# Starting the output products of a convolution layer before its last two units are finished

## The chip, the cores and the metric

The kernel runs on one core of a Trainium2 chip. The metric is the device time of one execution in microseconds (us). The profile is one execution taken by the hardware profiler; its engines are PE (matrix products; PEld is the loading of the stationary operand), DVE (vector), ACT (scalar activations), POOL (the third elementwise engine) and SP, whose queue issues the transfers (DMA).

## The reference, cut to what matters

Four layers transform 512 latent tokens and 256 context tokens of width 1024. Layers 0 and 3 are attention with low-rank keys, layer 1 is windowed attention, layer 2 is a Hyena layer, a gated long convolution. All end in a product with an output matrix, a norm and a gated residual:

```python
def hyena_mixer(hx, hc, w_in, conv_w, conv_b, ..., filt_bias, w_out, with_ctx_out):
    def run(h):
        p = h @ w_in
        u = short_conv(p[..., :(C_ORDER + 1) * C_WIDTH], conv_w, conv_b)
        gate = p[..., (C_ORDER + 1) * C_WIDTH:]
        v, *gx = jnp.split(u, C_ORDER + 1, axis=-1)
        z = v
        for o in range(C_ORDER):
            z = gx[o] * bidir_long_conv(z, filt[:, 0, o], filt[:, 1, o], filt_bias[o])
        return (z * jax.nn.silu(gate)) @ w_out
...
        x = x + gate_x * rmsnorm(yx, g_post[layer])
```

The last product sums over 1024 channels, so it needs every channel of `z * silu(gate)`.

## The kernel before, in words

**Layer 2.** `layer_C` works channel by channel in eight units of 128 channels, u = 0 to 7, over all 768 tokens. `w_in(u, c)` multiplies the hidden state `h` with the weights of one of four parts c (48 products a call, line 588), into one of the two double PSUM banks `pb`. `short(u, c)` adds the three-tap convolution (ACT line 1490, DVE lines 1495 to 1498). `gated(u)` is `short(u, 2)`, `w_in(u, 3)`, a SiLU (line 1577) and their product on POOL (line 1578). `conv(u, gx, kb, out)` is one long convolution: fold (DVE, 1506 and 1507), six transposes (PE, 1513), a split of each number into a high and a low part (341, 342), a sign flip (DVE, 1517), the forward transform (PE, 1525 and 1529), products with the filter's spectrum (DVE and POOL, 1534 to 1550), the inverse transform (PE, 1558 and 1563), and the sums that write `out` (ACT 1565 and 1566, DVE 1568 and 1569). It uses seven single PSUM banks `pa` in turn out of four, so two convolutions can overlap only in part. The result of unit u goes to `og[:, u]`.

**The tail of layer 2** (lines 1591 to 1617). Units 6 and 7 are interleaved: first convolutions 6a and 7a, then `gated(6)`, then second convolutions 6b (line 1599) and 7b (line 1600), the gate product of unit 6 (line 1601), `gated(7)`, and the gate product of unit 7 (line 1603). Then the blocks of `h` are freed, `self.W.pump(8, 8)` fetches and splits all eight 128-row blocks of the output matrix, the rings are freed, and `w_out_phase` runs.

**The output product.** `w_out_phase` goes over six tiles of 128 tokens. For a tile it splits the tile's columns of `og` into high and low (ACT 613, DVE 614; tile 0 in two pieces, units 0 to 5 and 6 to 7), then multiplies: for each unit k three products times two halves (line 622), 48 for a tile, into one `pb` bank, which `self.s()` hands out in turn. `post` normalizes (ACT 564, POOL 358 and 359, DVE 566, which reads and writes the bank, and 567, which reads it last), and `pre` prepares the next layer's input (eight transposes, line 543, among it).

**Weights.** `Stream` (`self.W`) fetches them in the order wanted. `_dma` (line 211) puts 512 KB into a staging slot of the F arena; `_split` copies the high part with ACT (line 230), takes the low part with POOL or DVE (line 233) and then frees the slot. `take` fetches and splits what is still missing; `cap_d` bounds the staged blocks and `cap_w` the split ones. A slot of the F arena is chosen among the first `turns_f` free ones, counted from the arena's top; the one freed longest ago is taken. With `turns_f = 1` it is always the topmost.

**Where the slots lie.** Following the arena's allocations through `layer_C` in the order of the code: the ring `acts` has blocks at words 6656, 11712 and 12496 of `arena_f` and one in `swing_F`; the last gate product of unit 7, `g7`, lies in the block 12496 to 13268. The ring `kr` of filter spectra holds words 8640 to 11712. As long as `kr` and `acts` are in use, one staging slot of 1024 words is free, at word 3072 of `swing_F`. Behind the layer the topmost slot of `arena_f` is 12736 to 13760, and so overlaps with `g7`'s block.

**What sets the order.** The last lines of `kernel` build the program in a `TileContext` with `schedule_with_timeline_sim=True`. It takes the code's order as a priority and lets an engine go on to later code where earlier code isn't ready. So `gated(7)`, behind 7b in the code, appears in the trace between the steps of 6b. Once built, the order on each engine is fixed.

Of the kernel before, what the change touches and what calls it, by code (L numbers as in the profile page):

```python
# [12 lines left out]
F32 = mybir.dt.float32  # L13
F32R = mybir.dt.float32r
BF16 = mybir.dt.bfloat16
AF = mybir.ActivationFunctionType
ALU = mybir.AluOpType
AX = mybir.AxisListType

P = 128  # L20
D = 1024
KD = 8
NX = 512
NC = 256
T = NX + NC
# [245 lines left out]
class Kern:  # L271
# [317 lines left out]

    W_AT_START = (4, 3, 3)  # L590

    def w_out_phase(self, L, og, wkey, order, last, hook):

        nc = self.nc
        self.W.cap_d, self.turns_f = 1, 1
        ws = [self.W.take((wkey, k), k < KD - 1) for k in range(KD)]
        h = None
        nxt = None if last else (L + 1) % 3
        ogv = og.v(KD, T)
        self.fill_to("g", L)  # L600
        self.turns_f = 6
        self.M.cap_d = self.M.look_d = 0
        xts = [self.load_x(L, order[0])]
        for n, t in enumerate(order):
            final = n == len(order) - 1
            if not final:
                xts.append(self.load_x(L, order[n + 1]))
            xt = xts[n]
            o2 = self.rs(2 * KD * P)
            ov = o2.v(2, KD, P)  # L610
            src = ogv[:, :, P * t:P * t + P]
            for k in (slice(0, 6), slice(6, 8)) if n == 0 else (slice(0, 8),):
                nc.scalar.activation(ov[:, 0, k], src[:, k], AF.Copy)
                nc.vector.tensor_tensor(ov[:, 1, k], src[:, k], ov[:, 0, k].bitcast(F32), op=ALU.subtract)
            if final:
                og.free()
            ys = self.s()
            for k in range(KD):
                wh, wl = ws[k][1]
                for q, (part, wt) in enumerate(((0, wh), (0, wl), (1, wh))):  # L620
                    for hf in range(2):
                        nc.tensor.matmul(ys[:, 512 * hf:512 * hf + 512], ov[:, part, k], wt[:, 0, 512 * hf:512 * hf + 512],  # L622
                                         start=(k == 0 and q == 0), stop=(k == KD - 1 and q == 2))
            o2.free()
            if n == 0:
                g = self.gates_out(L)
                if not last:
                    self.fill_to("ab", L + 1)
            if final:
                for blk, _ in ws:  # L630
                    blk.free()
                if nxt == 2:
                    self.set_swing("F")
                if nxt is not None:
                    self.W.cap_w, self.W.cap_d = self.W_AT_START[nxt], WD
                    self.W.pump(self.W.cap_w + 1, self.W.cap_w)
            self.post(L, t, ys, xt, g)
            if not last:
                if h is None:
                    h = self.h_alloc()  # L640
                self.pre(L + 1, t, xt, h)
            xt.free()
            if n == 1 and nxt == 0:
                self.W.cap_w, self.W.cap_d = 10, 1
                self.W.pump(2, 2)
            if n in (4, 5) and nxt == 2 and self.fillers and self.fillers[0][0] == "g":
                self.fill()
        if nxt is not None:
            self.W.pump(self.W.cap_w + 1, self.W.cap_w)
        for b in g:  # L650
            b.free()
        self.M.cap_d = self.M.look_d = 1
        return h
# [37 lines left out]
    def layer_A(self, L, j, h, ctx_out, last):  # L691
        nc, R, F = self.nc, self.R, self.F
        self.W.cap_w, self.W.cap_d, self.turns_f = 7, 3, 6
        qt = list(range(6)) if ctx_out else list(range(4))
        order = [0, 1, 2, 3, 4, 5]
        TQ = T if ctx_out else NX
        og = self.fl(KD * T)
# [276 lines left out]
            r.free()  # L974
        qr.free()
        kr.free()
        return self.w_out_phase(L, og, ("aw", L), order if not last else qt, last, None)


    def want_B(self, L, j):  # L980
# [21 lines left out]
    def layer_B(self, L, j, h, last):  # L1002
# [241 lines left out]
            r.free()  # L1244
        for x in (q, kx, vb):
            x.free()
        return self.w_out_phase(L, og, ("bw", L), order, last, None)


    def filters(self, j):  # L1250
# [182 lines left out]
    def layer_C(self, L, j, h, last):  # L1433
# [139 lines left out]
        def gated(u, sg=None):  # L1573
            g1 = short(u, 2)
            ps = w_in(u, 3)
            sg = ogv[:, u] if sg is None else sg
            nc.scalar.activation(sg, ps[:, 0:T], AF.Silu)
            nc.gpsimd.tensor_tensor(g1[:, 0:T], g1[:, 0:T], sg, op=ALU.mult)
            return g1
# [16 lines left out]
        conv(v7, g7, k7, ogv[:, 7])  # L1596
        k7 = load_k(15)
        g6 = gated(6, acts.next().ap[:, 0:T])
        conv(z, None, kb, ogv[:, 6])
        conv(ogv[:, 7], None, k7, ogv[:, 7])  # L1600
        nc.vector.tensor_tensor(ogv[:, 6], ogv[:, 6], g6[:, 0:T], op=ALU.mult)
        g7 = gated(7, acts.next().ap[:, 0:T])
        nc.vector.tensor_tensor(ogv[:, 7], ogv[:, 7], g7[:, 0:T], op=ALU.mult)
        for b in h:
            b.free()
        self.W.cap_w, self.W.cap_d = 8, 2
        self.lo_pool = None
        kr.free()
        self.W.cap_d = 3
        self.W.pump(8, 8)  # L1610
        self.lo_pool = True
        for r in (acts, fold, tr, zs, ubs, ybs):
            r.free()
        tb.free()
        tcf.free()
        self.set_swing("R")
        return self.w_out_phase(L, og, ("cw", L), order, last, None)


    def run(self, layers=(0, 1, 2, 3)):  # L1620
# [177 lines left out]
```

## Time and profile before

| what | value |
|---|---|
| median of 3 runs | 1949.14 us (1948.0 to 1954.3) |
| the profiled execution, its own time | 1953.32 us |
| its span, first to last instruction | 1951.5 us |
| mean granted PE clock | 0.984 |
| PE busy | 1820.0 us, 93% |
| DVE, ACT, POOL busy | 1182.5, 812.3, 521.6 us |

Layer 2 lies between about 1010 and 1594 us of the span. A row of the time line or of the chain begins with its start and its length, both in us. The row of a stretch gives, after the stretch's length, the busy time of each engine with the number of its instructions, then the clock that PE was granted, the share of DMA and its GB/s. A row of a group ends with its busy time, the mean ns of one instruction, and the idle time in front of it.

### The profile page before, as it was taken

How to read it: one execution, taken by the hardware profiler on the slowest of the kernel's cores; microseconds unless marked ns; L12 is line 12 of the kernel's file. 1: busy time of each engine (PE TensorE's matmuls, PEld its weight loads, DVE VectorE, ACT ScalarE, POOL GpSimd, SP SyncE). 2: the span in 40 equal slices, each digit the busy share in tenths (PEclk: the TensorE clock that was granted, in tenths of full speed). 3: DMA queues.
4: the chain of work that ended last, by engine and by line, in shares of the span. 5: the costliest groups of instructions: out<-in, count | busy, mean ns of one | idle time of the engine just before them, and what ended most of it. 6: DMA issues, size and time to landing. Idle time of an engine off the chain costs nothing.

```text
span 1951.5 us, 30304 instructions
## 1 busy us (share of the span) xinstructions
PE 1820.0 (93%) x11628; PEld 1576.6 (81%) x11628; DVE 1182.5 (61%) x2364; ACT 812.3 (42%) x1686; POOL 521.6 (27%) x523
## 2 busy tenths in 40 slices
PE   5879799999999899999989899999998998999998
PEld 3557588999988888888868699999987777889986
DVE  6684134787755367676675445566668553477663
ACT  3473132555544255565664422222222343354451
POOL 5561000000213321221231344444445221000120
PEclk9999899999999999999999999999999999999999
DMA  7857521001133112222362622222221335310121
GB/s 214 259 175 226 158 78 31 22 24 43 44 109 117 57 48 83 76 67 67 99 223 103 204 60 85 70 74 76 76 77 60 122 120 154 87 33 23 44 76 54
DMA packets 186356, 186.31 MB, mean 95 GB/s; under 512 B 16600, under 2 KB 164952, under 8 KB 186212
## 3 DMA queue, kind: packets, MB, share of 16 engines
q1 hardware_dynamic: 186212, 184.39, 30.6%
q8 instruction: 91, 1.49, 0.3%
q14 instruction: 53, 0.43, 0.1%
HBM read 160.24 MB, written 24.12 MB: 94 GB/s over the span
## 4 chain that ended last, share of the span: by engine, by line
PE 77%; DVE 10%; DMA 6%; ACT 3%; issue 3%; POOL 1%; SPq 0%; POOLq 0%; DVEq 0%; ACTq 0%
PE pb L588 13%; PE pb L622 11%; PE pa L588 10%; PE pb L873 5%; PE pa L912 4%; PE pa L1068 3%; PE pa L1049 3%; DMA arena_f<-in_w_mod_dram 3%; PE pa L1525 2%; PE pa L1558 2%; PE pa L442 2%; PE pa L898 2%; PE pa L1177 2%; PE pb L577 2%; PE pb L578 2%
## 5 line engine op out<-in xcount | busy, mean ns | idle before, releaser
L588 PE MATMUL pb<-arena_r 128*128 128x512 f32 (+1 forms) x1536 | 293.2, 345 | 8.1 <-DVE arena_f L1498 3.6
L588 PEld LDWEIGHTS pb<-arena_r 128*128 128x128 f32 x1536 | 239.3, 192 | 40.7 <-issue 3.8
L341 ACT ACTIVATE arena_r<-pa 128x384 fp32r<-128x384 f32 (+2 forms) x382 | 175.3, 478 | 198.5 <-PE pa L898 68.2
L342 DVE TENSOR_TENSOR arena_r<-pa,arena_r 128x384 fp32r<-128x384 f32 (+2 forms) x382 | 199.7, 537 | 86.6 <-ACT arena_r L341 84.9
L588 PE MATMUL pa<-arena_r,swing_R 128*128 128x512 f32 (+1 forms) x816 | 165.9, 355 | 0.6 <-DVE arena_r L342 0.4
L588 PEld LDWEIGHTS pa<-arena_r,swing_R 128*128 128x128 f32 x816 | 132.2, 188 | 21.8 <-DVE arena_r L342 0.6
L873 PE MATMUL pb<-arena_r 128*128 128x384 f32 (+1 forms) x720 | 141.4, 337 | 3.0 <-ACT arena_r L341 1.8
L233 POOL TENSOR_TENSOR swing_R<-arena_f,swing_R 128x1024 fp32r<-128x1024 f32 (+1 forms) x33 | 77.1, 2340 | 200.5 <-ACT swing_R L230 150.7
L873 PEld LDWEIGHTS pb<-arena_r 128*128 128x128 f32 x720 | 119.0, 188 | 5.1 <-ACT arena_r L341 2.5
L668 POOL TENSOR_TENSOR arena_f<-arena_f 128x128 f32<-128x128 f32 (+1 forms) x44 | 20.9, 474 | 364.1 <-DVE small L881 180.1
L622 PE MATMUL pb<-arena_r 128*128 128x512 f32 x480 | 115.2, 393 | 0.0
L358 POOL TENSOR_SCALAR small<-small 128x1 f32<-128x1 f32 x68 | 17.8, 262 | 349.1 <-ACT trash L564 135.6
L622 PEld LDWEIGHTS pb<-arena_r 128*128 128x128 f32 x480 | 89.5, 188 | 20.0 <-issue 1.1
L233 POOL TENSOR_TENSOR arena_r<-swing_F,arena_r 128x1024 fp32r<-128x1024 f32 x34 | 84.6, 2492 | 76.0 <-ACT arena_r L230 73.9
L912 PE MATMUL pa<-arena_r 128*128 128x256 f32 x624 | 91.4, 286 | 2.1 <-DVE arena_r L342 2.1
L912 PEld LDWEIGHTS pa<-arena_r 128*128 128x128 f32 x624 | 81.7, 190 | 4.8 <-ACT arena_r L341 2.5
L1068 PE MATMUL pa<-swing_R,arena_r 128*128 128x256 f32 x576 | 80.2, 289 | 5.1 <-DVE arena_f L348 3.8
L877 DVE TENSOR_REDUCE small<-pb 128x1 f32<-128x768 f32 (+1 forms) x80 | 67.5, 846 | 21.6 <-PE pb L873 20.7
L880 ACT ACTIVATE arena_f<-pb,small 128x768 f32<-128x768 f32 (+1 forms) x80 | 65.2, 816 | 32.9 <-DVE small L878 26.5
L1068 PEld LDWEIGHTS pa<-swing_R,arena_r 128*128 128x128 f32 x576 | 72.9, 192 | 7.3 <-DVE arena_f L348 5.2
L442 PE MATMUL pa<-arena_f,cst 128*32 128x256 f32 x744 | 57.0, 407 | 23.3 <-DMA arena_f<-in_w_mod_dram 23.0
L230 ACT ACTIVATE arena_r<-swing_F 128x1024 fp32r<-128x1024 f32 x34 | 36.2, 1063 | 101.5 <-PE pb L588 93.7
(266 smaller groups left out, 4239.6 us busy)
## 6 DMA issues: line engine op xcount, KB each, us to landing
arena_f<-in_w_mod_dram SPq DMA_DIRECT2D x93, 512.0 KB, 4.8
swing_F<-in_c_w_in_dram SPq DMA_DIRECT2D x31, 512.0 KB, 4.1
kd<-arena_f SPq DMA_DIRECT2D x48, 256.0 KB, 3.4
arena_f<-in_a_w_in_dram SPq DMA_DIRECT2D x24, 512.0 KB, 4.2
arena_f<-kd SPq DMA_DIRECT2D x16, 768.0 KB, 4.5
arena_f<-in_b_w_in_dram SPq DMA_DIRECT2D x20, 512.0 KB, 4.2
x<-arena_f SPq DMA_DIRECT2D x18, 512.0 KB, 4.1
arena_f<-in_a_w_out_dram SPq DMA_DIRECT2D x16, 512.0 KB
```

What stands on the lines that cost most here:

```text
L233: eng.tensor_tensor(lo, view, hi.bitcast(F32), op=ALU.subtract)
L341: self.nc.scalar.activation(hi, src, AF.Copy)
L342: self.nc.vector.tensor_tensor(lo, src, hi.bitcast(F32), op=ALU.subtract)
L442: nc.tensor.matmul(ps[32 * j:32 * j + 32, n0:n0 + 256], self.cst[:, 4 * kh + j, :], w[:, j, :], start=(kh == 0), stop=(kh == 1), skip_grou ...
L588: nc.tensor.matmul(out, l, rhs(part, k, i), start=(k == 0 and q == 0), stop=(k == kt - 1 and q == 2))
L622: nc.tensor.matmul(ys[:, 512 * hf:512 * hf + 512], ov[:, part, k], wt[:, 0, 512 * hf:512 * hf + 512], start=(k == 0 and q == 0), stop=(k = ...
L873: nc.tensor.matmul(S[:, 512 * b:512 * b + w], l, r[:, k0 + w * b:k0 + w * b + w], start=(q == 0), stop=(q == 4))
L877: nc.vector.tensor_reduce(mx, Sv, axis=AX.XY, op=ALU.max)
L880: nc.scalar.activation(pr.v(nb, w), Sv, AF.Exp, bias=mx, scale=sc, accum_out=sm)
L912: nc.tensor.matmul(o[:, 0:256], vv[:, a_, kt % 3, P * hh:P * hh + P], ptv[i // nh][:, b_, i % nh], start=(i == 0 and q == 0), stop=(i == n ...
L1049: nc.tensor.matmul(o, l[:, k], self.h_at(h, part, k, t0, n), start=(k == 0 and i == 0), stop=(k == KD - 1 and i == 2))
L1068: nc.tensor.matmul(ps[:, 0:256], self.h_at(h, part, k, P * t, P), w, start=(k == 0 and i == 0), stop=(k == KD - 1 and i == 2))
```

## The change

- The split and the products of one tile become a method, `w_out_tile`, that can do a range of units only.
- `gated(7)` moves ahead of 6b and 7b. The blocks of `h` are freed behind it, so ahead of these convolutions too. The caps become 6 split blocks and 2 staged ones.
- Behind 6b and 7b, but ahead of the two gate products of units 6 and 7, the first six blocks of the output matrix are taken and the products of units 0 to 5 are emitted for the first two tiles. Both `pb` banks hold these partial sums from then on.
- `pump(8, 8)` goes. `kr` is freed only after these products. The last two blocks are taken inside `w_out_phase`, under its `cap_d = 1` and `turns_f = 1`, behind `set_swing("R")`.
- For these two tiles `w_out_phase` adds units 6 and 7; the other four tiles go as before. The other two callers pass nothing and emit what they emitted.

```diff
-    def w_out_phase(self, L, og, wkey, order, last, hook):
+    def w_out_tile(self, og, ws, t, ks, part=None):
+        nc = self.nc
+        ogv = og.v(KD, T)
+        if part is None:
+            o2 = self.rs(2 * KD * P)
+            part = o2, self.s()
+        o2, ys = part
+        ov = o2.v(2, KD, P)
+        src = ogv[:, :, P * t:P * t + P]
+        nc.scalar.activation(ov[:, 0, ks], src[:, ks], AF.Copy)
+        nc.vector.tensor_tensor(ov[:, 1, ks], src[:, ks], ov[:, 0, ks].bitcast(F32), op=ALU.subtract)
+        for k in range(ks.start, ks.stop):
+            wh, wl = ws[k][1]
+            for q, (a, wt) in enumerate(((0, wh), (0, wl), (1, wh))):
+                for hf in range(2):
+                    nc.tensor.matmul(ys[:, 512 * hf:512 * hf + 512], ov[:, a, k], wt[:, 0, 512 * hf:512 * hf + 512],
+                                     start=(k == 0 and q == 0), stop=(k == KD - 1 and q == 2))
+        return part
+
+    def w_out_phase(self, L, og, wkey, order, last, begun=None):
         self.W.cap_d, self.turns_f = 1, 1
-        ws = [self.W.take((wkey, k), k < KD - 1) for k in range(KD)]
+        ws, parts, k0 = begun or ([], [], 0)
+        ws = ws + [self.W.take((wkey, k), k < KD - 1) for k in range(len(ws), KD)]
...
+            if n < len(parts):
+                o2, ys = self.w_out_tile(og, ws, t, slice(k0, KD), parts[n])
+            elif n == 0:
+                part = self.w_out_tile(og, ws, t, slice(0, 6))
+                o2, ys = self.w_out_tile(og, ws, t, slice(6, KD), part)
+            else:
+                o2, ys = self.w_out_tile(og, ws, t, slice(0, KD))
...
         g6 = gated(6, acts.next().ap[:, 0:T])
+        g7 = gated(7, acts.next().ap[:, 0:T])
+        for b in h:
+            b.free()
+        self.W.cap_w, self.W.cap_d = 6, 2
+        self.lo_pool = None
         conv(z, None, kb, ogv[:, 6])
         conv(ogv[:, 7], None, k7, ogv[:, 7])
+
+        ws = [self.W.take((("cw", L), k), k < 3) for k in range(6)]
+        parts = [self.w_out_tile(og, ws, t, slice(0, 6)) for t in order[:2]]
         nc.vector.tensor_tensor(ogv[:, 6], ogv[:, 6], g6[:, 0:T], op=ALU.mult)
-        g7 = gated(7, acts.next().ap[:, 0:T])
         nc.vector.tensor_tensor(ogv[:, 7], ogv[:, 7], g7[:, 0:T], op=ALU.mult)
-        for b in h:
-            b.free()
-        self.W.cap_w, self.W.cap_d = 8, 2
-        self.lo_pool = None
         kr.free()
-        self.W.cap_d = 3
-        self.W.pump(8, 8)
         self.lo_pool = True
...
-        return self.w_out_phase(L, og, ("cw", L), order, last, None)
+        return self.w_out_phase(L, og, ("cw", L), order, last, (ws, parts, 6))
```

More of the change, by code (lines that the diff above doesn't have):

```diff
@@ L590 @@
     W_AT_START = (4, 3, 3)
-    def w_out_phase(self, L, og, wkey, order, last, hook):
+    def w_out_tile(self, og, ws, t, ks, part=None):
[17 more added lines that the diff above has]
+    def w_out_phase(self, L, og, wkey, order, last, begun=None):
         nc = self.nc
         self.W.cap_d, self.turns_f = 1, 1
-        ws = [self.W.take((wkey, k), k < KD - 1) for k in range(KD)]
+        ws, parts, k0 = begun or ([], [], 0)
+        ws = ws + [self.W.take((wkey, k), k < KD - 1) for k in range(len(ws), KD)]
         h = None
         nxt = None if last else (L + 1) % 3
-        ogv = og.v(KD, T)
         self.fill_to("g", L)
@@ L608, in w_out_phase @@
             xt = xts[n]
[L609 to L614, printed above, removed]
+            if n < len(parts):
[5 more added lines that the diff above has]
+                o2, ys = self.w_out_tile(og, ws, t, slice(0, KD))
             if final:
                 og.free()
[L617 to L623, printed above, removed]
             o2.free()
@@ L976, in layer_A @@
         kr.free()
-        return self.w_out_phase(L, og, ("aw", L), order if not last else qt, last, None)
+        return self.w_out_phase(L, og, ("aw", L), order if not last else qt, last)
     def want_B(self, L, j):
@@ L1246, in layer_B @@
             x.free()
-        return self.w_out_phase(L, og, ("bw", L), order, last, None)
+        return self.w_out_phase(L, og, ("bw", L), order, last)
     def filters(self, j):
```

## The prediction

> **What bounds the kernel now.** I read the page first, then a table of stretches over the end of layer 2, the waits there, the chain of work that ended last, and the time line.
>
> ```profile
> span 1951.5 us, 30304 instructions
> ...
> PE 1820.0 (93%) x11628; PEld 1576.6 (81%) x11628; DVE 1182.5 (61%) x2364; ACT 812.3 (42%) x1686; POOL 521.6 (27%) x523
> ```
>
> PE is the bound, 93% busy, so a change can win only where PE stands still or runs slowly. The stretches show where that is around the change:
>
> ```profile
> 1462.00:1492.70 30.70, 29.41 (x202) 26.91 (x200) 24.61 (x37) 8.74 (x13) 13.84 (x11) 1.00 0.14 43
> 1492.70:1521.60 28.90, 20.28 (x107) 15.46 (x105) 24.45 (x33) 9.02 (x15) 15.39 (x10) 0.88 0.34 109
> 1521.60:1594.40 72.80, 72.48 (x322) 57.19 (x322) 37.33 (x47) 30.25 (x52) 13.17 (x23) 1.00 0.33 113
> ```
>
> The first is nearly full: the input products of `gated(7)` fill the holes of 7a and 6b. The third, the output products, is full. In the second, where the end of 6b and all of 7b are left, PE is idle for 28.9 - 20.3 = 8.6 us, and its clock of 0.88 takes another 0.12 x 28.9 = 3.5 us. These 12 us, 0.6% of the time, are all that there is to win. The waits of that stretch are links of the convolution's own chain through DVE, with no other product at hand:
>
> ```profile
> PE pa L1558 <- DVE arena_r L1544: 4.0, 3, 1.8
> ...
> PE pa L1525 <- DVE arena_r L1517: 2.4, 1, 2.4
> ```
>
> **The moved gates.** The chain shows the products of `gated(7)` (line 588) between the steps of 7a and 6b:
>
> ```profile
> 1467.01 0.72 PE pa L1529 x6
> 1467.73 4.83 PE pb L588 x27
> ...
> 1476.05 1.92 PE pa L1558 x16
> 1477.97 0.89 PE pa L1563 x8
> 1478.86 0.22 PE pa L1513 x2
> 1479.08 5.55 PE pb L588 x32
> 1484.63 2.88 PE pa L1525 x24
> ...
> 1502.12 2.90 PE pa L1525 x12
> ```
>
> Before, 6b stands ahead of `gated(7)` in the code, and its forward transform starts at 1484.63. Now `gated(7)` is ahead. What that does to a convolution shows at 6a, which stands behind four `short` calls:
>
> ```profile
> 1412.53 0.28 DVE L1507 TENSOR_TENSOR swing_F<-swing_F 128x128 f32<-128x128 f32 x1
> ...
> 1425.98 0.69 DVE L1548 TENSOR_TENSOR swing_F<-pa,arena_f 128x512 f32<-128x512 f32 x1
> ```
>
> ```profile
> 1433.71 3.48 PE pb L588 x20
> 1437.19 0.66 PE pa L1513 x6
> ```
>
> Its fold is done by 1412.8, and its first banks are read out by 1426.7 (line 1548 of the convolution ahead). Yet its transposes wait until 1437.19, when the input products ahead of them are through. So I take it that 6b now waits for all of `gated(7)`: 96 products at 5.55/32 = 0.174 us are 16.7 us, from 1467.7, with 7a's inverse transform among them (24 x 1.92/16 + 0.89 = 3.8 us). That ends at 1488.2, and 6b's transposes (0.66) at 1488.9. From there to its forward transform I need the split and the sign flip:
>
> ```profile
> 1480.06 2.37 DVE L1517 TENSOR_SCALAR arena_r<-arena_r,sgn 128x1536 fp32r<-128x1536 f32 x1
> ```
>
> Before, the transposes ended at 1479.08 and the flip at 1482.43, 3.4 us later. So 6b's forward transform starts at 1492.3, 7.7 us late. From there to 7b's it took 1502.1 - 1484.6 = 17.5 us, which I keep. The end of 7b:
>
> ```profile
> 1520.47 0.96 DVE L1603 TENSOR_TENSOR arena_f<-arena_f 128x768 f32<-128x768 f32 x1
> ```
>
> ```profile
> 1500.00:1510.00 10.00, 6.28 (x32) 5.28 (x32) 7.59 (x8) 2.71 (x4) 5.37 (x4) 0.83 0.23 62
> 1510.00:1520.00 10.00, 7.43 (x36) 5.62 (x36) 8.08 (x10) 2.53 (x6) 5.68 (x4) 0.83 0.58 200
> ```
>
> The last gate product ends at 1521.4, 19.3 us behind 7b's forward transform. Both stretches of 10 us there had a clock of 0.83, 0.17 x 10 = 1.7 us lost in each. With products to fill its holes PE stays warm; about half of the chain is on PE, so I take off 1.7 and have 17.6. The last gate product then ends at 1492.3 + 17.5 + 17.6 = 1527.4, 6.0 us later than before. Ends for this: 0 later, if 6b's transposes slip in at their old place, and 9 later, if every step of 7b also loses a microsecond behind filling products.
>
> **The early products.** They are 2 tiles x 6 units x 6 = 72:
>
> ```profile
> 1546.57 10.08 PE pb L622 x42
> ```
>
> At 0.24 us each, 17.3 us leave the full third stretch. Between 1488.2 and 1527.4, 39.2 us, PE then has two convolutions at 8.0 us (2.88 + 0.72 forward, 3.8 inverse, 0.66 transposes), and these 17.3, so 33.3 us, beside the small products of the gates: the holes are mostly filled, as the change says. The splits of their operands are these, three pieces in a row:
>
> ```profile
> 1520.76 2.09 ACT L613 ACTIVATE swing_R<-arena_f 128x768 fp32r<-128x768 f32 x3
> ...
> 1522.48 2.42 DVE L614 TENSOR_TENSOR swing_R<-arena_f,swing_R 128x768 fp32r<-128x768 f32 x3
> ```
>
> Two of the wider pieces go to DVE earlier, under 0.9 us each; DVE has 28.9 - 24.5 = 4.4 us free in the second stretch. Ahead of them in the code stand the convolutions, so I take nothing, and keep 2 us for the range. Tile 1 gets one split more on ACT and DVE, hidden in the wait below.
>
> **The last two weight blocks.** This is where the win goes. With `cap_d = 1` and `turns_f = 1` block 6 is staged in the topmost slot, words 12736 to 13760. That slot overlaps with `g7`, which the last gate product reads. The trace has a load into this very slot, the next layer's first:
>
> ```profile
> 1515.22 1.46 SPq L211 DMA_DIRECT2D arena_f<-in_c_w_out_dram  x2
> ...
> 1521.45 0.38 SPq L211 DMA_DIRECT2D arena_f<-in_a_w_in_dram  x1
> ```
>
> It is issued at 1521.45, when line 1603 has ended (1521.43). Now this is block 6, and block 7 follows through the same slot, once block 6 is split. The steps:
>
> ```profile
> arena_f<-in_c_w_out_dram SPq DMA_DIRECT2D x5, 512.0 KB, 3.5
> ```
>
> ```profile
> L233 POOL TENSOR_TENSOR arena_r<-swing_F,arena_r 128x1024 fp32r<-128x1024 f32 x34 | 84.6, 2492 | 76.0 <-ACT arena_r L230 73.9
> ...
> L230 ACT ACTIVATE arena_r<-swing_F 128x1024 fp32r<-128x1024 f32 x34 | 36.2, 1063 | 101.5 <-PE pb L588 93.7
> ```
>
> A block takes 3.5 + 1.1 + 2.5 = 7.1 us (`lo_pool` is True again, so POOL takes the low part), two take 14.2, all behind the end of 7b; before, the last two were issued at 1515.22 and behind it, ahead of that end. Four more products of tile 0 (1.0 us) need block 7's low part or follow those that do. Nothing else can run: both `pb` banks hold tiles 0 and 1, and tile 2 needs the first of them, so it waits for `post`:
>
> ```profile
> 1534.40 1.02 ACT L564 ACTIVATE trash<-pb 128x1024 bf16<-128x1024 f32 x1 [9.21 <-PE pb L622]
> ...
> 1537.78 1.22 DVE L567 TENSOR_TENSOR arena_f<-arena_f,pb 128x1024 f32<-128x1024 f32 x1
> ```
>
> From 1534.4 to 1539.0, 4.6 us. Before, this was hidden under tile 1's 48 products (11.5 us); that cover is gone. In these gaps the clock falls; I take one loss of 1.7 us, the size seen above. Tile 2 starts 14.2 + 1.0 + 4.6 + 1.7 = 21.5 us behind the last gate product, at 1548.9.
>
> The Trainium skill, "TensorE: Matmul & The Clock Gate", section "What's actually happening", says that one idle window of about 3.4 us halves the clock until a busy one has passed. By it all three gaps would cost, not one; this is a rival below. The 0.83 above agrees with a halving for a third of each stretch.
>
> **The sum.** Tiles 2 to 5 are 192 products x 0.24 = 46.1 us, and five `pre` put their transposes among them:
>
> ```profile
> 1544.46 1.03 PE L543 MATMUL pa<-ident,arena_f 128*128 128x128 f32 x8
> ...
> 1582.72 11.79 PE L622 MATMUL pb<-arena_r,swing_R 128*128 128x512 f32 x48
> ```
>
> That is 5.2 us. The output products end at 1548.9 + 46.1 + 5.2 = 1600.2; before, they ended at 1582.72 + 11.79 = 1594.5. So +5.7 us, and the start of layer 3 moves along, since its loads wait for slots that `post` and `pre` free. The profiled execution of 1953.32 us (span 1951.5 and 1.8 around it) would become 1959.0; it lies 4.2 us above the median of 1949.14, so for the median I say 1954.8. Dropping `pump`, the caps and the other callers cost nothing: the first six blocks come through the slot in `swing_F`, 7.1 us each, four of them between 1488 and 1517.
>
> **The rivals.**
>
> *Slower: PE stuck behind an early product.* The order on PE is fixed when the program is built. Blocks 2 to 5 pass one slot, so block 3 is ready about 1488.2 + 3.6 + 7.1 = 1498.9, block 4 at 1506, block 5 at 1513. If a product on one of them was put ahead of a step of 6b or 7b and its block lands later than planned, PE and the convolution wait. For it: two convolutions' chain is all that counts there, and DVE and POOL, which take the low parts, are busy. Against: input weights came through the same slot all through the layer without a hole in PE (the first stretch). One wait of 5 us, under a full step of 7.1, gives +10.7, 1959.8. It decides as soon as it is over 0.2 us, since a measurement of this kernel can tell about 0.3%, 5.8 us, from no change.
>
> *Slower: the clock falls in all three gaps* (behind the last gate product 4.6 us, between blocks 6 and 7 as much, and during `post` 4.6). Twice 1.7 more give +9.1, 1958.2. Against: the products that the second gap slows are few.
>
> *No change: 6b isn't held up.* If its transposes slip between the products of `gated(7)` and the warm clock makes up the rest, the last gate product ends where it did, at 1521.4: 1521.4 + 21.5 + 51.3 = 1594.2, -0.3 us, 1948.8. For it: gaps in readiness let later code in often. Against: 6a's 10 us wait.
>
> *Faster: blocks 6 and 7 are there in time*, if the slot isn't the one that I followed. Then tile 0 needs a split (under 1 us), 12 products (2.9) and `post` (4.6): tile 2 starts at 1527.4 + 8.5 = 1535.9, and the end is 1587.2, -7.3 us, 1941.8. Against: the load at 1521.45. That the early products don't get into the holes at all would give about no change as well, and counts with the case above.
>
> **The numbers.** Forecast 0.38, with its own range 1950 to 1959 (0 to 9 us for the delay of 7b, 2 for DVE, 2 for the loads): 0.24 of it within 0.3%, 0.14 above. 6b not held up: 0.20, within. PE stuck: 0.19 and cold clock: 0.08, both slower. Blocks in time: 0.15, faster. So faster 0.15, same 0.44, slower 0.41. The range is 1942 to 1962: it takes in the stuck queue, most of its spread, and the faster case's middle, and leaves out some 2 in 10.
>
> **What would show it.** Right: line 1525 of 6b starts near 1492, the idle of 8.6 us is gone from the convolutions, PE is near full until about 1527; the load of `in_c_w_out` comes right behind line 1603, a second one 7 us later; PE then stands for over 10 us in three pieces, and tile 2 starts 20 us behind line 1603. Wrong: 6b's transposes inside `gated(7)`; loads of the last blocks ahead of line 1603; waits of PE for line 230 or 233 ahead of that line (the stuck queue); an end of layer 2 that moves by less or more than 0 to 9 us.

## The result, and the profile after

| | before | after | ratio [95% interval] |
|---|---|---|---|
| median | 1948.57 us (1947.02 to 1954.3, 4 runs) | 1968.95 us (1964.54 to 1973.15, 4 runs) | 1.0087 [1.0062, 1.0112] |
| the same change run again | 1950.80 us | 1965.27 us (1962.34 to 1972.28, 6 runs) | 1.0078 [1.0061, 1.0095] |
| profiled execution, its span | 1953.32, 1951.5 us | 1964.54, 1962.7 us | |
| mean granted PE clock | 0.984 | 0.979 | |

The change costs 14 to 20 us where +5.7 was forecast, and both medians lie above 1962, the upper end of the forecast's range. Ratios compare undisturbed runs: one of the seven runs of the kernel called "one product" below took 5581.86 us and is left out of its ratio. The page of the kernel after starts like this:

```profile
span 1962.7 us, 30306 instructions
...
PE 1824.4 (93%) x11628; PEld 1579.8 (80%) x11628; DVE 1172.6 (60%) x2364; ACT 812.4 (41%) x1687; POOL 525.2 (27%) x524
```

The two profiled executions differ already ahead of the change: the last store of layer 1 (line 568), in code that is the same, is issued 6.1 us earlier in the kernel after. From here on times of different kernels are therefore counted from that store; its row before, then after:

```profile
1094.91 0.34 SPq L568 DMA_DIRECT2D x<-arena_f  x1
```

```profile
1088.85 0.34 SPq L568 DMA_DIRECT2D x<-arena_f  x1
```

| us from the last store of layer 1 | before | after | difference | forecast |
|---|---|---|---|---|
| end of the last gate product | 426.5 | 434.1 | +7.6 | +6.0 |
| tile 2's first product | 450.4 | 456.5 | +6.1 | +3.6 |
| end of the output products | 499.6 | 510.1 | +10.5 | +5.7 |
| end of the span | 856.6 | 873.9 | +17.3 | +5.7 |

Lines of the kernel after: the products are line 608 (622 before), their split 602 and 603 (613, 614), the convolution's transposes 1527 (1513), forward transform 1539 (1525) and sign flip 1531 (1517), unit 7's gate product 1624 (1603). Its time line over the moved gates and the early products:

```profile
1472.46 9.51 PE L588 MATMUL pb<-arena_r 128*128 128x256 f32 x54
...
1481.80 0.82 PE L1527 MATMUL pa<-ident,swing_F 128*128 128x128 f32 x6
...
1482.86 4.91 PE L608 MATMUL pb<-arena_r 128*128 128x512 f32 x20 [0.24 <-ACT arena_f L1591]
...
1486.49 1.01 DVE L1531 TENSOR_SCALAR arena_r<-arena_r,sgn 128x1536 fp32r<-128x1536 f32 x1
...
1487.61 3.08 PE L1539 MATMUL pa<-arena_r 128*128 128x256 f32 x24
...
1501.97 5.73 PE L608 MATMUL pb<-arena_r 128*128 128x512 f32 x24
...
1503.95 1.02 DVE L1531 TENSOR_SCALAR arena_r<-arena_r,sgn 128x1536 fp32r<-128x1536 f32 x1
...
1507.54 3.04 PE L1539 MATMUL pa<-arena_r 128*128 128x256 f32 x24
```

6b's six transposes stand right behind the last products of `gated(7)`, as foreseen. Early products fill what follows. Before 7b's forward transform they do a little more: the flip is done at 1504.97, but 24 early products keep PE until 1507.7, and the transform starts 2.6 us after it could.

Behind the last gate product the time line shows the two late blocks, one after the other, and then the wait for a bank:

```profile
1521.97 0.96 DVE L1624 TENSOR_TENSOR arena_f<-arena_f 128x768 f32<-128x768 f32 x1
...
1523.01 0.33 SPq L211 DMA_DIRECT2D arena_f<-in_c_w_out_dram  x1
...
1526.93 1.06 ACT L230 ACTIVATE swing_R<-arena_f 128x1024 fp32r<-128x1024 f32 x1 [3.24 <-DMA arena_f<-in_c_w_out_dram]
...
1528.06 2.37 POOL L233 TENSOR_TENSOR swing_R<-arena_f,swing_R 128x1024 fp32r<-128x1024 f32 x1 [9.84 <-ACT swing_R L230]
...
1530.46 0.33 SPq L211 DMA_DIRECT2D arena_f<-in_c_w_out_dram  x1
...
1537.48 3.62 PE L608 MATMUL pb<-swing_R,arena_r 128*128 128x512 f32 x8 [1.25 <-POOL swing_R L233]
1539.59 1.02 ACT L564 ACTIVATE trash<-pb 128x1024 bf16<-128x1024 f32 x1 [4.61 <-PE pb L608]
...
1542.85 1.22 DVE L603 TENSOR_TENSOR arena_r<-arena_f,arena_r 128x1024 fp32r<-128x1024 f32 x1
1543.98 1.22 DVE L567 TENSOR_TENSOR arena_f<-arena_f,pb 128x1024 f32<-128x1024 f32 x1
...
1545.34 8.40 PE L608 MATMUL pb<-arena_r 128*128 128x512 f32 x24 [4.25 <-DVE arena_f L567]
```

The first load is issued at 1523.01, 0.08 us behind the gate product that reads its slot; the second at 1530.46, when block 6 is split. The first 24 products of tile 2 take 8.40 us, 0.35 each, where 0.24 is the warm rate. The stretches, cut at the last gate product and at tile 2:

```profile
1472.00:1492.00 20.00, 19.75 (x120) 17.22 (x120) 11.22 (x23) 5.62 (x8) 6.79 (x4) 1.00 0.19 63
1492.00:1522.93 30.93, 27.53 (x158) 22.21 (x156) 16.92 (x29) 6.61 (x12) 9.82 (x9) 1.00 0.23 76
1522.93:1545.34 22.41, 10.84 (x25) 6.82 (x25) 5.60 (x8) 4.95 (x8) 5.48 (x4) 0.67 0.29 94
1545.34:1598.91 53.57, 51.75 (x226) 41.32 (x227) 27.04 (x36) 25.55 (x45) 14.36 (x22) 0.95 0.34 113
```

The holes of 7b are smaller (3.4 us idle instead of 8.6) and the clock there is 1.00 instead of 0.88: the early products do what the change says. Then come 22.4 us in which PE works 10.8, at a clock of 0.67.

The rest of the loss lies where the change edits nothing. From the end of the output products to the end of the span, layer 3, it is 357.0 us before and 363.8 after. The first 60 us of it, PE's waits before, and after:

```profile
PE pa L710 <- DVE arena_f L707: 2.9, 2, 2.1
PE pb L577 <- DVE arena_f L567: 2.2, 1, 2.2
PE pa L750 <- ACT arena_r L746: 1.6, 1, 1.6
```

```profile
PE pa L724 <- DVE arena_f L721: 5.4, 3, 2.9
PE pb L577 <- DVE arena_f L567: 2.4, 1, 2.4
PE pa L764 <- ACT arena_r L760: 1.8, 1, 1.8
```

and the same 60 us as a stretch, before, and after:

```profile
1594.51:1654.51 60.00, 52.34 (x340) 44.68 (x339) 28.36 (x56) 24.19 (x55) 12.22 (x31) 0.97 0.51 149
```

```profile
1598.91:1658.91 60.00, 49.63 (x308) 42.66 (x308) 26.48 (x53) 22.23 (x51) 10.91 (x28) 0.89 0.47 141
```

PE is idle 2.7 us longer, most of it at the transposes for the low-rank keys (lines 724 and 764; 710 and 750 before), and the clock of 0.89 against 0.97 takes up to 0.08 x 60 = 4.8 more. Together that is about the whole 6.8 us. The waits that are new stand some 45 us behind the output products:

```profile
1643.41 0.42 PE L579 MATMUL pb<-arena_r 128*128 128x320 f32 x1
1646.00 0.44 PE L724 MATMUL pa<-ident,arena_f 128*128 128x128 f32 x2 [2.17 <-DVE arena_f L721]
1648.19 0.47 PE L764 MATMUL pa<-ident,arena_r 128*128 128x128 f32 x1 [1.75 <-ACT arena_r L760]
```

The transposes stand right behind these products on PE, so PE waits out the norm in between, and then the copy of line 760. Behind these two holes PE has half its clock for 6.8 us, from 1646.6. The kernel before has holes of 0.76 and 1.64 us there, and 3.4 us at half clock. The first products of line 588 in layer 3, before and after:

```profile
1651.54 1.56 PE L588 MATMUL pa<-arena_r,swing_R 128*128 128x512 f32 x6
```

```profile
1662.67 1.56 PE L588 MATMUL pa<-arena_r,swing_R 128*128 128x512 f32 x6
```

They start 57.0 us behind the output products before (1651.54 - 1594.51) and 63.8 after (1662.67 - 1598.91); from there to the end both kernels take the same time.

### The profile page after: what moved, and what is told of

It is laid out like the page before. It is cut to its first block, busy times and chain, and to the rows that moved or that the text cites. A ratio compares the mean times of both kernels' runs of the same rounds, so it can differ in the third digit from the quotient of the medians.

```text
span 1962.7 us, 30306 instructions
## 1 busy us (share of the span) xinstructions
PE 1824.4 (93%) x11628; PEld 1579.8 (80%) x11628; DVE 1172.6 (60%) x2364; ACT 812.4 (41%) x1687; POOL 525.2 (27%) x524
## 3 DMA queue, kind: packets, MB, share of 16 engines
q8 instruction: 91, 1.49, 0.3%
## 5 line engine op out<-in xcount | busy, mean ns | idle before, releaser
L588 PEld LDWEIGHTS pb<-arena_r 128*128 128x128 f32 x1536 | 238.8, 191 | 40.6 <-issue 3.8
L608 PE MATMUL pb<-arena_r 128*128 128x512 f32 x696 | 170.6, 399 | 6.3 <-DVE arena_f L567 4.2
L608 PEld LDWEIGHTS pb<-arena_r 128*128 128x128 f32 x696 | 130.9, 191 | 37.4 <-issue 5.9
L887 PEld LDWEIGHTS pb<-arena_r 128*128 128x128 f32 x720 | 119.0, 188 | 5.1 <-ACT arena_r L341 2.5
L608 PE MATMUL pb<-swing_R,arena_r 128*128 128x512 f32 x360 | 96.5, 415 | 7.3 <-ACT swing_R L230 5.7
L608 PEld LDWEIGHTS pb<-swing_R,arena_r 128*128 128x128 f32 x360 | 69.0, 196 | 26.8 <-ACT swing_R L230 7.2
L891 DVE TENSOR_REDUCE small<-pb 128x1 f32<-128x768 f32 (+1 forms) x80 | 67.5, 846 | 21.5 <-PE pb L887 20.7
```

Source lines behind the costliest of these rows:

```text
L588: nc.tensor.matmul(out, l, rhs(part, k, i), start=(k == 0 and q == 0), stop=(k == kt - 1 and q == 2))
L608: nc.tensor.matmul(ys[:, 512 * hf:512 * hf + 512], ov[:, a, k], wt[:, 0, 512 * hf:512 * hf + 512], start=(k == 0 and q == 0), stop=(k == K ...
L887: nc.tensor.matmul(S[:, 512 * b:512 * b + w], l, r[:, k0 + w * b:k0 + w * b + w], start=(q == 0), stop=(q == 4))
L891: nc.vector.tensor_reduce(mx, Sv, axis=AX.XY, op=ALU.max)
```

## The experiments

Two questions were open. What do the moved gates, the early products and the late blocks each cost, and why does layer 3 pay? Where the first expectations name a theory A, it is the prediction's own: the last two blocks come too late. All positions are in the table behind the experiments.

**Slots of `kr` for the last two blocks.** In `w_out_phase`:

```diff
-        self.W.cap_d, self.turns_f = 1, 1
+        self.W.cap_d, self.turns_f = 1, 6 if begun else 1
```

> The changed kernel, but the last two weight blocks are staged in any of six free slots, the longest free first, so in the two halves of the filter ring, which are read out some 8 us ahead of the last gate product. Theory A (these blocks come too late): both loads are issued ahead of the last gate product, tile 2 starts about 12 us behind it, not 22.4, and some 10 us of the 17 lost are won back: about 1.004 of the kernel before. Theory B (the moved gates hold up the last two convolutions, and that is most of it): within 3 us of the changed kernel, 1.008. Theory C (two tiles hold both banks, so tile 2 waits for the first tile's norm): that wait of 4 to 6 us is still there, at most 2 us won.

Measured: 1950.32 us, 0.9995 [0.9984, 1.0006]. Both loads now go out long ahead of the last gate product:

```profile
1502.47 13.96 SPq L211 DMA_DIRECT2D arena_f<-in_c_w_out_dram  x2
```

The output products end 10.3 us earlier than in the changed kernel, and layer 3 is back at 356.1 us. Tile 2 starts 8.2 us earlier, 14.6 us behind the last gate product, where theory A had 12, and the wait of theory C for the bank is still there, 4.85 us. So the slot decides; but more came back than the late blocks account for.

**One more block ahead.**

```diff
-        self.W.cap_d, self.turns_f = 1, 1
+        self.W.cap_d, self.turns_f = 2 if begun else 1, 1
```

> The changed kernel, the last two weight blocks through the one late slot as before, but a second block may be staged, so that the first block of layer 3's weights is loaded behind them, some 15 us earlier than in the changed kernel. If the 6.6 us lost behind the output products come from that late load, 4 to 6 us are won back, ratio about 1.006; if they come from PE's clock and from a shift of all loads, it stays within 2 us of the changed kernel, 1.008 to 1.009.

Measured: 1960.77 us, 1.0045 [1.0029, 1.0061]. The last two blocks come as late as in the changed kernel (tile 2 at 455.4), and yet the output products end 3.2 us earlier, with 13.7 us at half clock between the last gate product and tile 3 where the changed kernel has 20.5. The same waits, then, do not fix what follows them. The block of layer 3 is issued even ahead of the last two, 402.5 us behind the store of layer 1 instead of 459.4, and layer 3 takes 358.6 us, 5.2 less than in the changed kernel, as the theory of the late load has it. But PE's order in layer 3 differs from the changed kernel's too, so this run can't tell the load from the order.

**The gates behind the convolutions.** `gated(7)`, the freeing of `h` and the caps move behind 6b and 7b; the blocks stay late.

```diff
-        g7 = gated(7, acts.next().ap[:, 0:T])
...
         conv(z, None, kb, ogv[:, 6])
         conv(ogv[:, 7], None, k7, ogv[:, 7])
+        g7 = gated(7, acts.next().ap[:, 0:T])
...
```

> The changed kernel, but the gates of unit 7 stand behind both second convolutions in the code again; the early products stay. Theory B: the forward transform of 6b starts about 8 us earlier, the last gate product 6 to 8 us earlier, and that much is won back: about 1.005 of the kernel before. Theory A: the last two blocks are loaded behind the last gate product as ever and tile 2 starts 20 to 22 us behind it, so no more than these 6 to 8 us. If the early products alone were a win, it would be under 1.000.

Measured: 1951.59 us, 1.0003 [0.9989, 1.0017]. The last gate product ends 4.7 us earlier than in the changed kernel, less than the 6 to 8 of theory B and still 2.9 later than before, the output products end 6.7 earlier, and layer 3 takes 352.9, less than before. Each of the two repairs alone thus wins back nearly everything, which terms that simply add up can't do; the table's last column but one has a part of the answer, layer 3, whose order both change in the same way.

**The gates alone.** In the kernel before, `gated(7)` goes ahead of 6b and 7b, and nothing else.

```diff
+        g7 = gated(7, acts.next().ap[:, 0:T])
         conv(z, None, kb, ogv[:, 6])
         conv(ogv[:, 7], None, k7, ogv[:, 7])
         nc.vector.tensor_tensor(ogv[:, 6], ogv[:, 6], g6[:, 0:T], op=ALU.mult)
-        g7 = gated(7, acts.next().ap[:, 0:T])
```

> The kernel before, with one edit: the gates of unit 7 stand ahead of the last two convolutions in the code. Theory B: 6b and 7b run later by 6 to 8 us with nothing to fill their holes, so 6 to 8 us slower than before, 1.003 to 1.004. If the order of the code doesn't hold up 6b, within 2 us of before.

Measured: 1962.02 us, 1.0048 [1.0031, 1.0065]. The last gate product ends 9.9 us late, more than the 6 to 8 expected, and all behind it moves by 10. That is more than the 7.6 us with early products; but in the kernel without early products below, whose gates are ahead too, it is 6.5, so these runs don't show whether early products raise or lower what the moved gates cost.

**One tile early.** `order[:1]` in place of `order[:2]`; gates ahead, blocks late.

> The change, but only tile 0's products begin early; tile 1's 36 products of units 0 to 5 stay behind the last gate product. By the theory of the late weight blocks these 36 (8.7 us at 0.24) fill the waits for blocks 6 and 7, so PE idles about 1 us there instead of 7.4, but tile 2 can start no sooner, since the blocks set it: tile 2 as in the changed kernel or 2 us earlier by a warmer clock, and the output products end 0 to 4 us earlier. By the theory that the layer behind is slower because of the order in which its instructions were planned, the 6.8 us of layer 3 go as well, since that order is here almost the one of the experiment with slots of kr: ratio to the kernel before 1.003 to 1.005. If layer 3's loss comes with late blocks and not with that order, the ratio is 1.006 to 1.009.

Measured: 1957.88 us, 1.0043 [1.0028, 1.0058], as the theories of the late blocks and of the order say together: tile 2 at 454.7, 1.8 us earlier than in the changed kernel, layer 3 at 356.3. The 36 products that were moved early bought nothing: behind the last gate product they would have run in a wait.

**No early products.** Gates ahead, blocks late, and all 48 products of each tile behind the gate products.

```diff
-        parts = [self.w_out_tile(og, ws, t, slice(0, 6)) for t in order[:2]]
...
-        return self.w_out_phase(L, og, ("cw", L), order, last, (ws, parts, 6))
+        return self.w_out_phase(L, og, ("cw", L), order, last, (ws, [], 0))
```

> The change without its early products: the gates are still ahead, blocks 6 and 7 are still taken inside the output phase, but all 48 products of each tile stand behind the last gate product. By the theory that the early products took the cover from the late blocks, both loads now land under 72 products (17 us) and cost nothing: tile 2 starts about 10 us later than in the kernel before, as with the gates alone, layer 3 takes about 357 us, ratio 1.004 to 1.006. If late blocks cost by themselves, tile 2 starts 16 us later than before and the ratio is 1.008 to 1.011.

Measured: 1956.06 us, 1.0034 [1.0023, 1.0045], just below the range of the theory of the cover; tile 2 starts 5.9 us later than in the kernel before, not 10. The blocks are as late as ever, but PE hardly waits for them (it is idle for 0.7 us between the last gate product and tile 2, in the changed kernel for 11.6):

```profile
1522.30 8.73 PE L608 MATMUL pb<-arena_r,swing_R 128*128 128x512 f32 x36
...
1522.36 0.33 SPq L211 DMA_DIRECT2D arena_f<-in_c_w_out_dram  x1
...
1529.45 0.33 SPq L211 DMA_DIRECT2D arena_f<-in_c_w_out_dram  x1
```

The products of units 0 to 5 run under the loads, and tile 2 starts at 456.3, where it starts in the changed kernel with 72 products done beforehand. With late blocks the early products win no time: they turn the cover of the loads into idle time.

**Both costs undone: gates behind, slots of `kr`.** The third and the first edit together.

> The change with both of its costs undone: the gates of unit 7 behind the two convolutions, and the last two blocks staged in slots that are free in time. The planned order of layer 3's first products is here the very one of the changed kernel. By the theory that late blocks and their waits make layer 3's start slow, tile 2 starts some 6 us earlier than in the kernel before, the output products end 4 to 6 us earlier, layer 3 takes 353 to 357 us as before: ratio 0.996 to 0.998. By the theory that the planned order of layer 3 makes it slow, the output products end as early, but layer 3 takes about 363 us, and the ratio is 1.000 to 1.002.

Measured: 1954.22 us, 1.0022 [1.0009, 1.0035], a little above what the theory of the order gave. The output products end 3.0 us earlier than before, yet layer 3 takes 362.9 us. Its waits in the first 60 us:

```profile
PE pa L724 <- DVE arena_f L721: 6.3, 3, 3.9
...
PE pa L764 <- ACT arena_r L760: 1.8, 1, 1.8
```

These are the changed kernel's waits, without a late block. What the two kernels share is the order in which the first 420 products of layer 3 stand on PE: by line, tiles and shapes each is the same, while place by place the changed kernel and the first experiment agree in 0.77 of them, the first experiment and the kernel before in 0.73. That order is the scheduler's, planned ahead from its own model of the time.

**Spare products in the waits.** In `w_out_tile`, ahead of unit k of the two begun tiles, 36 in all:

```diff
+            if warm[k - 6]:
+                pw = self.a()
+                for _ in range(warm[k - 6]):
+                    nc.tensor.matmul(pw, ov[:, 0, 6], ws[0][1][0][:, 0, 0:512], start=True, stop=True)
```

> The change with 36 products more that write to a spare bank and are read by nobody: 12 in each wait behind the last gate product (for block 6, between the blocks, and behind tile 1's last unit), so that PE is busy there. It waits for the same blocks. By the theory that the clock's fall in these waits costs beyond the waits, the half-clock stretches between the last gate product and tile 3 go, tile 2's first 24 products take 5.8 us instead of 8.4, and the output products end 3 to 5 us earlier than in the changed kernel; if that is all, the ratio is about 1.006. Layer 3's planned order differs from the changed kernel's too, and by the theory of the order layer 3 gives back 3 to 7 us: ratio 1.003 to 1.005. If the clock doesn't matter, the output products end no earlier than in the changed kernel, or up to 3 us later: 1.009 to 1.011.

Measured: 1961.39 us, 1.0065 [1.0046, 1.0085], an interval that overlaps with those of the change. Of 20.5 us at half clock between the last gate product and tile 3, 6.8 are left, and the output products end 2.9 us earlier, a little less than expected: the scheduler put all 36 ahead of the last 20 products of tiles 0 and 1, and the wait for the bank stayed empty, so that tile 2 still started cold (8.07 us for its first 24 products). That the clock is what the 2.9 us are isn't shown: 1.4 of them are a wait of PE ahead of tile 3 that this kernel doesn't have, and the kernels with one more block ahead and with one product, which fill no wait, end these products 3.2 and 2.4 us earlier as well. Layer 3, in yet another order, takes 361.6 us, 2.2 less than in the changed kernel where 3 to 7 were expected.

**One product.** The changed kernel with one such spare product, ahead of unit 6 of tile 0.

> The change and one product more (0.24 us), written to a spare bank behind the last gate product and read by nobody. It moves the scheduler's plan: up to the end of the output products the order on TensorE is the changed kernel's but for that product and 7 others, while layer 3 starts in the order that the experiment with slots of kr has. By the theory that layer 3's planned order costs it 6 to 7 us, the output products end where the changed kernel ends them and layer 3 takes 353 to 357 us instead of 364: ratio 1.004 to 1.006. By the theory that layer 3 starts slowly because blocks and loads come late, nothing changes: 1.008 to 1.010, as for the change run again beside it.

Measured: 1959.01 us, 1.0047 [1.0029, 1.0066], beside 1965.27, 1.0078 [1.0061, 1.0095], of the change run again. Layer 3, now in the order of the first experiment, takes 355.9 us instead of 363.8; the output products end 2.4 us earlier, which wasn't expected. Blocks and gates are as late as in the changed kernel. Where that has its two holes, other products stand between here, and the transposes (line 728 in this kernel) don't wait:

```profile
1640.69 1.93 PE L442 MATMUL pa<-arena_f,cst 128*32 128x256 f32 x32
...
1644.05 0.38 PE L728 MATMUL pa<-ident,arena_f 128*128 128x128 f32 x2
```

The loads of layer 3's weights ahead of this place aren't what differs: they go out 41.7 us behind the output products here (1641.82 - 1600.12) and 42.1 in the changed kernel (1641.03 - 1598.91).

**One product in the repaired kernel.** The kernel with gates behind and slots of `kr`, and the same spare product.

> The kernel with the gates behind and the slots of kr, and one product more to a spare bank, which puts layer 3's start into the order of the experiment with slots of kr. By the theory of the order, its 4 us loss against the kernel before turns into a win: output products 3 us earlier than before, layer 3 not slower than before: ratio 0.997 to 0.999. If the order doesn't matter, 1.001 to 1.003 as without that product.

Measured: 1944.36 us, 0.9967 [0.9954, 0.9981]: faster than both kernels. Against the 1.0022 without it one product of 0.24 us wins 0.55%. Layer 3 takes 353.5 us instead of 362.9, and its first 60 us show neither of the two late holes at the low-rank keys. The 2.9 us at line 728 are a wait some 16 us behind the output products that every one of these kernels has, of 2.0 to 3.9 us:

```profile
PE pa L728 <- DVE arena_f L725: 2.9, 1, 2.9
PE pb L577 <- DVE arena_f L567: 2.6, 1, 2.6
```

```profile
1588.92:1648.92 60.00, 53.67 (x346) 46.77 (x346) 28.17 (x55) 23.16 (x53) 11.16 (x30) 0.97 0.47 142
```

**One tile early in the repaired kernel.** Gates behind, slots of `kr`, `order[:1]`.

> Gates behind, slots of kr, and only tile 0's products early. Tile 1's 48 products then cover the wait for tile 0's bank (4.9 us with two tiles early), so the output products end 3 to 6 us earlier than before. Layer 3's order is almost that of the experiment with slots of kr, so layer 3 takes no longer than before: ratio 0.996 to 0.999. If the early products win only as many as they are, 36 instead of 72 bring nothing over the kernel before: 0.999 to 1.001.

Measured: 1948.22 us, 0.9988 [0.9978, 0.9997]. The wait of 4.9 us for the bank is gone, but the output products end only 1.7 us earlier than before, not 3 to 6: 36 products more are left behind the gate product. The ratio fits both theories of its expectation at their common edge. Layer 3 takes 358.4 us, 1.4 more than before, in an order that agrees with the first experiment's in 0.77 of the first 420 places. The profiled execution has a clock of 0.936, since its record has 0.95 where the others have 1.00, but its products are no slower: from tile 3's first product to the end of the output products it is 36.6 us here and 36.7 in the kernel before.

**The change again.**

> The changed kernel as it is, for the interval beside the three others: every theory expects 1.0087 within 0.0025, and layer 3 at 361 to 365 us with the same two holes at its rank products.

Measured: 1.0078 [1.0061, 1.0095], every stage within 0.4 us of the first profile, and layer 3 again at 363.8 us.

The positions, all in us from the last store of layer 1, from one profiled execution each; layer 3 is from the end of the output products to the end of the span:

| kernel | last gate product ends | tile 2 starts | output products end | layer 3 | ratio |
|---|---|---|---|---|---|
| before | 426.5 | 450.4 | 499.6 | 357.0 | |
| the change | 434.1 | 456.5 | 510.1 | 363.8 | 1.0087 |
| the change again | 434.5 | 456.8 | 510.4 | 363.8 | 1.0078 |
| slots of `kr` | 433.6 | 448.3 | 499.8 | 356.1 | 0.9995 |
| one more block ahead | 434.0 | 455.4 | 506.9 | 358.6 | 1.0045 |
| gates behind | 429.4 | 450.6 | 503.4 | 352.9 | 1.0003 |
| gates alone | 436.4 | 460.3 | 510.0 | 356.9 | 1.0048 |
| one tile early | 433.5 | 454.7 | 506.7 | 356.3 | 1.0043 |
| no early products | 433.0 | 456.3 | 505.8 | 357.2 | 1.0034 |
| gates behind, slots of `kr` | 428.8 | 445.0 | 496.6 | 362.9 | 1.0022 |
| spare products | 434.6 | 455.8 | 507.2 | 361.6 | 1.0065 |
| one product | 433.5 | 455.4 | 507.7 | 355.9 | 1.0047 |
| gates behind, `kr`, one product | 428.8 | 442.3 | 493.9 | 353.5 | 0.9967 |
| gates behind, `kr`, one tile | 429.0 | 448.2 | 497.9 | 358.4 | 0.9988 |

The three kernels whose layer 3 takes 363 us have the changed kernel's order there, and no other kernel has it. The four in the order of the first experiment (it, gates behind, and the two with one product) lie at 352.9 to 356.1; the kernel before and the gates alone share a third order (in 0.99 of the places), 357.0 and 356.9.

## Why the prediction was wrong

**The step that failed most: "the start of layer 3 moves along".** It gave layer 3 nothing, and layer 3 took 6.8 of the 11.6 us by which the sum was short. The reason put behind it, that layer 3's loads wait for slots that the end of layer 2 frees, isn't what counted. The scheduler plans the order of layer 3's first products together with all that stands ahead, and the change led it to an order with two holes at the low-rank keys, 2.17 and 1.75 us, and 6.8 us at half clock behind them. That the order is the cause is shown from both sides: the same order without late blocks costs the same (362.9), and one product that changes the order gives the time back in both kernels, with the blocks late or in time. In the medians the one product is worth 6.3 us (1965.27 to 1959.01) and 9.9 us (1954.22 to 1944.36), of which the output products, 2.4 and 2.7 us earlier, have a part. Why the scheduler's model prefers this order stays open.

The other 4.8 us lie ahead of layer 3: 1.6 up to the last gate product, 0.9 from there to tile 2, and 2.3 from tile 2 to the end of the output products, which took 53.6 us where 46.1 + 5.2 were forecast.

**The clock, a term that was too small.** The prediction took one loss of 1.7 us for the three gaps. The stretch up to tile 2 ran at 0.67. Most of that is hidden in the wait for the blocks, but the four products between block 7 and `post` took 2.1 us (1537.48 to 1539.59) where 1.0 was counted, and tile 2's first 24 products 8.40 - 24 x 0.24 = 2.6 us more. The rival with a fall of the clock in all three gaps gave +9.1 for the output products; they measured +10.5, with 1.6 us of that from the gates, which the rival didn't have. Its condition was right: the clock fell in all three gaps. The rows that spoke for one loss only were taken from a stretch in which PE was never idle for long.

**The moved gates: right in mechanism, 1.6 us short.** 6b's transposes stand behind all of `gated(7)`, at 393.8 from the store by its end (1482.62 - 1088.85), where 1488.9 - 1094.9 = 394.0 was foreseen. The flip came 1.5 us later than the 3.4 us taken, since DVE does the gate's taps in between; 7b's forward transform lost 2.6 us to early products; and its end gained more from the warm clock than the 1.7 us taken: from the transform to the last gate product 15.4 us instead of 17.6. So the 1.6 us are what is left of larger errors that partly cancel. With the gates in their old place and the early products there, the last gate product still ends 2.9 us late; for that the forecast took nothing and kept 2 us in its range.

**The late blocks: right.** The slot, the load right behind line 1624, two passes of 7.4 and 7.0 us where 7.1 each were taken. The wait for the bank took 5.6 us (1539.59 to 1545.20) instead of 4.6, because tile 2's split on DVE (line 603) got between the two halves of `post` (lines 566 and 567). Tile 2 started 22.4 us behind the last gate product; the forecast was 21.5.

**The early products: the price was right, the sign of the saving was not asked.** They fill the holes. But the prediction took them as 17.3 us won and the wait of 14.2 us as the price beside it, without asking what the wait would have been without them. It would have been almost nothing: without early products PE is idle for 0.7 us between the last gate product and tile 2, and the output products end at 505.8, with them at 510.1.

**The rivals.** PE stuck behind an early product: it happened, but as 2.6 us behind 24 products that were ready, not behind one whose block was missing. 6b not held up: no. Blocks in time: as a kernel it measured 0.9995, not -7.3 us. There 24 products and a `post` (1540.4 - 1525.8 = 14.6 us from the last gate product to tile 2) stand where 8.5 were taken, since tile 1's last 12 products and the splits run first, and the gates stay 7 us late. Only with the gates behind, too, and layer 3 in a good order does it win.

## What to carry to other kernels

Work that covers a load is not free to be moved: before filling a hole with it, ask what will cover the load it leaves, and put the slot question (which slot, who reads it last) first. Where a scheduler plans the order, an edit changes the order of code far behind it; compare that order before giving a later stage "moves along", and try a neutral edit of one instruction before believing a difference of half a per cent. Idle time on the bounding engine is to be priced with the clock that it costs the next products.

## What the runs showed of the hardware

The clock of PE follows a grid of 3.4 us, and what it is in one stretch depends on the stretch before. The changed kernel behind the last gate product, cut along that grid (stretch, length, PE's busy time first; the clock is the third number from the right):

```profile
1520.35:1523.75 3.40, 1.49 (x3) 0.30 (x2) 2.88 (x6) 0.72 (x2) 0.00 (x0) 0.99 0.03 5
1523.75:1527.15 3.40, 0.00 (x0) 0.00 (x0) 0.42 (x2) 0.22 (x1) 0.00 (x0) 0.50 0.72 207
1527.15:1530.55 3.40, 2.14 (x5) 1.23 (x5) 0.72 (x2) 0.84 (x1) 2.37 (x1) 0.50 0.28 101
1530.55:1533.95 3.40, 3.40 (x8) 2.41 (x8) 0.57 (x1) 0.03 (x1) 0.00 (x0) 0.50 0.43 154
1533.95:1537.35 3.40, 1.43 (x5) 0.67 (x4) 0.00 (x0) 1.03 (x1) 2.30 (x1) 1.00 0.00 0
1537.35:1540.75 3.40, 3.27 (x8) 2.48 (x8) 0.00 (x0) 1.16 (x3) 0.07 (x1) 0.50 0.44 154
1540.75:1544.15 3.40, 0.35 (x2) 0.00 (x0) 2.50 (x3) 0.90 (x1) 0.74 (x2) 1.00 0.00 0
1544.15:1547.55 3.40, 2.21 (x5) 1.84 (x6) 1.22 (x2) 2.24 (x4) 0.74 (x2) 0.51 0.38 154
1547.55:1550.95 3.40, 3.40 (x9) 2.67 (x8) 2.65 (x3) 0.03 (x1) 1.06 (x2) 0.50 0.33 96
```

After a stretch with 3.27 or 3.40 us of work the clock is 1.00, after one with 2.21 or less it is 0.50. A stretch need not be empty for that: 1.49 us of work, 44%, were not enough at the start. So a gap of 3 us can bring half clock for the next 3.4 us, or for longer where those are again too thin to count as busy, or not at all, by where it falls on the grid: the wait at line 577 behind the output products took 2.4 us in the changed kernel and brought 3.4 us at half clock, and with the slots of `kr` it took 3.1 us and brought none.

Over thirteen of the fourteen profiles (without "gates behind, `kr`, one tile", whose record has 0.95 for the full clock), each cut along its own grid, no stretch at full clock in which PE was busy for more than 0.64 of the time was followed by half clock, and none below 0.45 by full clock; in between both occur. At half clock no stretch below 0.77 was followed by full clock.

Where the grid lies is luck. Counted from the span's start, its phase is between 0.1 and 3.3 us in the fourteen profiles; in the two of the changed kernel it is 1.4 and 1.7, so that they agree within 0.4 us says little about the spread. The program up to the last store of layer 1, with the same order on PE in all fourteen, takes 1088.8 to 1096.2 us. How much of that is the grid isn't shown, but 2 or 3 us between two single profiles need not come from an edit.

The Trainium skill, "TensorE: Matmul & The Clock Gate", section "What's actually happening", has the two speeds, the window of about 3.4 us and that it runs freely; the traces agree, but for the 0.95 of that one execution. By its words an idle window lowers the clock; in the rows above, windows 42 and 44% busy lowered it as well, and at half clock windows 63 and 65% busy kept it low.
